# First feed-forward layers with the activations stationary: 60 of 88 pairs on one core

## The chip, the core and the metric

The kernel runs on one NeuronCore of a Trainium2 chip. The metric is device time in microseconds (us) from one launch, shorter is better. The kernel before takes 2496.74 us (median of three runs, 2496.37 to 2496.89). The engines named below are PE (TensorE, the matrix products; its weight loads have a row of their own, PEld), DVE (VectorE), ACT (ScalarE), POOL (GpSimd) and SP (SyncE, which issues most transfers).

## What is computed

One block of a model with 256 tokens and 2048 features: a feed-forward layer, a mixer (attention beside a gated delta rule), and a second feed-forward layer, each with an adaptive shift and scale before it and a gated residual and layer norm behind it. The change is in the feed-forward layers:

```
def swiglu_ffn(h, w_in, w_out):              # h [256, 2048], w_in [2048, 2 * 5632], w_out [5632, 2048]
    g, u = jnp.split(h @ w_in, 2, axis=-1)
    return (jax.nn.silu(g) * u) @ w_out
...
y = swiglu_ffn(x * (1.0 + scale[:, 0]) + shift[:, 0], w_ffn_in[l, 0], w_ffn_out[l, 0])
x = layer_norm(DEEPNORM_ALPHA * x + 0.5 * gate[:, 0] * y, ln_g[l, 0], ln_b[l, 0])
```

## The kernel before

**Numbers in two parts.** Every large product is made of three: an operand is split into a rounded part `hi` and a rest `lo`, and `mm3` (L145) issues hi·hi, hi·lo and lo·hi, one after the other, into one accumulator in PSUM; they stand in the profile as L147, L148 and L149. Weights come from HBM in chunks of 512 KB, `raw` [128, 1024]. ACT rounds a chunk to `hi` and DVE (in some stages POOL) subtracts to get `lo` (`_split`, L177). There are five `raw` buffers and three pairs of `hi` and `lo` (WB = 3), so the split of a chunk can start only when PE is through with the chunk three before it.

**Two forms of product.** `_wstat` (L274) keeps weights stationary: 128x128 weights are loaded into PE and 256 columns, all tokens of h^T, stream past them. A chunk is 24 such products, each with its own weight load. The result has features on the partitions. In the profile these are `mm<-h_hi,hi` and the like: out <- streaming operand, stationary operand. `_xstat` (L287) keeps activations stationary, 128 features by 128 tokens, and 512 weight columns stream. A chunk is 12 products, and the result has tokens on the partitions; two accumulators of [128, 512], one for each half of the tokens, fill side by side. In the profile these are `mx<-hi,hid`: the streaming weights first, then the stationary activations.

**Stages.** The hidden 5632 features of a feed-forward layer are 44 pairs of a gate block and an up block of 128 features. A layer runs in two halves (SIZES, L31: 28 and 16 pairs in layer 0, 22 and 22 in layer 2). A half first makes its pairs, then multiplies all of them with the second weights in `_y_blocks` (L702), in four blocks of 512 columns by `_xstat` with `hid` stationary. The first 28 pairs of layer 0 are made in a special way, by feature tiles as h becomes known (`start`, tiles `mms`), and do not change. The other 60 pairs are made by `_wstat`, four chunks a pair, tiles `mm`; two pairs of layer 2 (tiles `pre`) are made while the layer norm before it still produces h (`_Next.rest`, L569).

**Behind a pair.** `_ffn_hid_run` (L737) reads the pair's bank: ACT takes silu of the gate half (`sg`), DVE multiplies with the up half (`hidf`), ACT rounds to `hid` hi and DVE subtracts to `hid` lo. Features are on the partitions already, which is what `_y_blocks` wants of its stationary operand.

**Order.** It is set at build time: one main stream of products, and threads (`_Thread`, `spawn`) that put their instructions between them when a rough clock says that they are due. Each engine then runs its own list strictly in the order in which it was written. `weights` (L219) has the splits of the next two chunks written ahead of the products of a chunk. Four banks (`psm`) serve the main stream, and four (`pss`, tiles named `sm` in the code) serve threads. `_Ada` (L357) computes vectors for later parts between the products, on DVE, from 512 KB transfers of its own (`ar`): in layer 0 mostly reductions of 128x1024 against `crow`, in layer 2 sums into `acc` for one gate.

**Placement.** In both kernels the built program puts h (hi and lo) at byte 18016 and byte 34400 of each partition, behind the 4-byte tile `eps`; both are 32 past a multiple of 64. `hid`, `mgh`, `mgl`, `hi` and `lo` all start at multiples of 64.

Of the kernel before, what the change touches and what calls it, by code (L numbers as in the profile page):

```python
# [8 lines left out]
F32 = mybir.dt.float32  # L9
# [9 lines left out]
S = 256  # L19
# [11 lines left out]
SIZES = {0: (28, 16), 2: (22, 22)}  # L31
# [43 lines left out]
class _Engine:  # L75
    """An engine, with a rough clock of when it is through with what it was given."""
# [15 lines left out]
class _Kernel:  # L92
# [35 lines left out]
    def bank(self, shape, name):  # L128
        """A bank for a job of the main stream, when the thread that reads it last is through."""
        if len(self.users) == 4:  # L130
            th = self.users.pop(0)
            if th is not None:
                self.wait(lambda: th.done)
        self.users.append(None)
        return self.psm.tile(shape, F32, tag="mm", name=f"{name}{self.uid()}")

    def read(self, gen, back=1):
        """A thread that reads the newest bank (or the one back)."""
        th = self.spawn(gen)
        self.users[-back] = th  # L140
        return th

    # products
# [56 lines left out]
    def ahead(self, upto):  # L200
        """Emit loads and splits so that chunks up to upto are under way."""
# [9 lines left out]
    def hold(self, first, n):  # L211
        """The parts of n chunks go where h was."""
# [6 lines left out]
    def weights(self, held=0):  # L219
        """Parts of the next chunk; held: chunks before it whose products come later."""  # L220
# [27 lines left out]
def _rsqrt(k, pool, y, x, tag):  # L248
    """y = x ** -0.5 for small tiles: a guess from the exponent, then Newton's steps."""
# [9 lines left out]
def _products(k, ps, w, kt0, nkt, acts, first, last):  # L259
    """ps[:, b, :] += W[:, b]^T act, weights stationary, for nkt feature tiles."""  # L260
# [13 lines left out]
def _wstat(k, n, acts):  # L274
    """Two output blocks [128, 256] side by side in one bank, from n chunks."""
# [10 lines left out]

def _xstat(k, n, act, done, tail=0):  # L287
    """Natural [2][128 tok, 512]: activations stationary, weights moving; done: what reads it.

    tail: the last chunks go token tile by token tile and half by half (a bank for each), and are  # L290
    read at once."""
# [8 lines left out]
    def part(c, w, j, t, i):  # L300
        kt = 2 * c + j
        act.need(k, kt)
        lo, hi = halves[i]
        sl = slice(j * 512 + lo, j * 512 + hi)
        tk = slice(t * 128, (t + 1) * 128)
        k.mm3(pss[t][i][:, lo:hi], (_tile(act[0], kt)[:, tk], _tile(act[1], kt)[:, tk]), (w[0][:, sl], w[1][:, sl]),
              start=(kt == 0), stop=(kt == 2 * n - 1))
        k.pump()
# [25 lines left out]

def _ada_row(k, pool):
    """silu(c) along the columns of all partitions (in PSUM), from features on partitions."""
# [5 lines left out]
def _ada_keep(k):  # L342
    """The same in SBUF, for what comes later."""
# [6 lines left out]
def _ada_dot(k, raw, half, sub, kind, f, tmp, d):  # L350
    """One half of the sums for 128 features of a shift or a scale; features on partitions."""
# [83 lines left out]
class _More:  # L435
    """Shifts and scales whose weights are part of the weight stream."""
# [13 lines left out]
def _affine(k, sub, ln, shT, scT):  # L450
    """A = g (1 + scale), B = b (1 + scale) + shift, features on partitions."""
# [41 lines left out]
def _h_tile(k, pool, h, f, src, A, B):  # L493
    """h^T tile f = src * A + B, split in two parts."""
# [14 lines left out]

class _Ln:  # L510
    """Layer norm of x by rows: the statistics, and what comes of them."""
# [8 lines left out]
    def table(self):  # L520
        """Has the table of the square root there in time."""
# [7 lines left out]
    def factors(self, t):  # L529
        """1 / std, - mean / std and - mean."""  # L530
# [14 lines left out]
class _Next:  # L545
    """The layer norm, with x of it to DRAM and h of the next part, and that part's first products."""

    def __init__(self, k, idx, prep):
        self.k, self.idx, self.prep = k, idx, prep
# [19 lines left out]
    def rest(self, ln):  # L569
# [39 lines left out]
        th.step()  # L609
        acts = [h, h]  # L610
# [8 lines left out]
class _Last:  # L619
    """The layer norm of the result."""  # L620
# [4 lines left out]
    def load(self):  # L625
        """Thread: its vectors, for all tokens."""
# [36 lines left out]
def _load_x(k, a, pool, rows, tags, idx, delay, pace):  # L663
    """Thread: the residual from DRAM, with the affine part of the layer norm before it."""
# [22 lines left out]
def _residual(k, n, t, ps, lo, hi, gate, first, st):  # L687
    """x = (first: alpha) x + 0.5 gate y for columns lo..hi of 512; statistics if st."""
# [13 lines left out]
def _y_blocks(k, nchunk, act, ada, sub, first, ln, finish, tail):  # L702
    """y = act W2 by blocks of 512 columns, into x; with ln, also the layer norm after it."""
# [55 lines left out]

def _ffn(k, a, h, sub, items, interval, start, pre, finish, tail):  # L760
# [941 lines left out]
```

## Time and profile before

| | us |
|---|---|
| median of three runs | 2496.74 (2496.37 to 2496.89) |
| span of the profiled execution | 2501.1 |
| PE busy (products) | 2356.6, 94% |
| PEld busy (weight loads, beside PE) | 2230.8, 89% |
| DVE busy | 1747.1, 70% |
| ACT busy | 1037.8, 41% |
| POOL busy | 582.9, 23% |

The profile is of one execution of the program; its times are from the span's start. A product shows as busy from its first column to the modelled end of its last, so neighbours overlap: the pace of a stage is the distance from one start to the next, not the duration. The changed stages are from 565.81 to 750.13 us (16 pairs of layer 0), from 1723.99 to 1991.14 us (22 pairs of layer 2, the first two of them beside the layer norm) and from 2110.84 to 2364.29 us (the other 22).

### The profile page before, as it was taken

The numbers are of one execution on the slowest core, as the hardware profiler recorded it, in microseconds if no ns is written. First come the engines' busy times: TensorE is split into PE (matmuls) and PEld (weight loads), VectorE is DVE, ScalarE is ACT, GpSimd is POOL, SyncE is SP. The second block draws the span as 40 slices with busy tenths as digits, with TensorE's granted clock in tenths as the row PEclk, the third lists the DMA queues.
The fourth block names the chain that finished last, engine by engine and source line by source line (L and its number), as shares of the span: only waits on it lengthen the run. The fifth ranks groups of instructions, "written<-read, shape, count | busy, mean of one in ns | idle before, by whom it ended". The sixth has DMA issues, their size and how long they took to land. (4 is left out here: it accounts for less than half of the span.)

```text
span 2501.1 us, 42377 instructions
## 1 busy us (share of the span) xinstructions
PE 2356.6 (94%) x16989; PEld 2230.8 (89%) x16989; DVE 1747.1 (70%) x2436; ACT 1037.8 (41%) x1420; POOL 582.9 (23%) x320
## 2 busy tenths in 40 slices
PE   7999889789999889998988999998999999999997
PEld 7999887679998878898888999988999988999987
DVE  5767998577776567878686798786687555444456
ACT  4434334234443443444434434434444433444433
POOL 5885761000000443423334040004030000000001
PEclk8999999899999999999999999999999999999999
DMA  9998657788886555544445988885888665555553
GB/s 360 331 335 292 234 193 252 210 318 306 299 303 210 177 180 166 176 162 140 144 156 163 321 285 307 281 290 195 279 297 303 205 195 191 184 185 180 184 193 127
DMA packets 166245, 582.05 MB, mean 233 GB/s; under 512 B 19692, under 2 KB 22676, under 8 KB 165280
## 3 DMA queue, kind: packets, MB, share of 16 engines
q1 hardware_dynamic: 166048, 579.34, 68.3%
q8 instruction: 133, 2.18, 0.4%
q14 instruction: 64, 0.52, 0.1%
HBM read 571.41 MB, written 7.86 MB: 232 GB/s over the span
## 5 line engine op out<-in xcount | busy, mean ns | idle before, releaser
L88 ACT ACTIVATE hi<-raw 128x1024 fp32r<-128x1024 f32 x768 | 810.9, 1058 | 1019.1 <-PE mm L148 406.6
L88 DVE TENSOR_TENSOR lo<-raw,hi 128x1024 fp32r<-128x1024 f32 x587 | 735.7, 1257 | 507.7 <-ACT hi L88 504.3
L149 PE MATMUL mm<-h_hi,lo 128*128 128x256 f32 x3072 | 869.7, 283 | 19.1 <-DVE lo L88 19.0
L147 PE MATMUL mm<-h_hi,hi 128*128 128x256 f32 x3072 | 879.8, 286 | 0.0
L148 PE MATMUL mm<-h_lo,hi 128*128 128x256 f32 x3072 | 870.4, 283 | 0.0
L88 POOL TENSOR_TENSOR lo<-raw,hi 128x1024 fp32r<-128x1024 f32 x181 | 448.1, 2486 | 1030.3 <-ACT hi L88 1009.9
L149 PEld LDWEIGHTS mm<-h_hi,lo 128*128 128x128 f32 x3072 | 584.8, 190 | 21.1 <-DVE lo L88 20.7
L147 PEld LDWEIGHTS mm<-h_hi,hi 128*128 128x128 f32 x3072 | 582.3, 190 | 2.9 <-issue 2.5
L148 PEld LDWEIGHTS mm<-h_lo,hi 128*128 128x128 f32 x3072 | 582.6, 190 | 0.9 <-issue 0.6
L148 PE MATMUL mx<-lo,hid 128*128 128x512 f32 (+1 forms) x764 | 285.0, 373 | 25.3 <-DVE lo L88 23.5
L149 PE MATMUL mx<-hi,hid 128*128 128x512 f32 (+1 forms) x764 | 284.4, 372 | 0.0
L147 PE MATMUL mx<-hi,hid 128*128 128x512 f32 (+1 forms) x764 | 284.2, 372 | 0.1
L149 PE MATMUL mms<-h_hi,lo 128*128 128x256 f32 x896 | 258.9, 289 | 14.0 <-POOL lo L88 14.0
L147 PE MATMUL mms<-h_hi,hi 128*128 128x256 f32 x896 | 258.5, 288 | 9.6 <-ACT hi L88 6.5
L148 PE MATMUL mms<-h_lo,hi 128*128 128x256 f32 x896 | 256.7, 287 | 2.2 <-POOL h_lo L88 2.2
L148 PEld LDWEIGHTS mx<-lo,hid 128*128 128x128 f32 x764 | 144.8, 190 | 51.3 <-DVE lo L88 24.2
L88 DVE SCALAR_TENSOR_TENSOR acc<-ar,cs,acc 128x512 f32<-128x512 f32 x180 | 186.1, 1034 | 5.7 <-DMA ar<-in_w_gate_dram 2.0
L149 PEld LDWEIGHTS mms<-h_hi,lo 128*128 128x128 f32 x896 | 173.0, 193 | 15.7 <-POOL lo L88 15.7
L147 PEld LDWEIGHTS mms<-h_hi,hi 128*128 128x128 f32 x896 | 173.9, 194 | 10.7 <-ACT hi L88 7.5
L148 PEld LDWEIGHTS mms<-h_lo,hi 128*128 128x128 f32 x896 | 175.0, 195 | 2.7 <-POOL h_lo L88 2.5
L147 PEld LDWEIGHTS mx<-hi,hid 128*128 128x128 f32 x764 | 144.9, 190 | 26.0 <-issue 0.6
L149 PEld LDWEIGHTS mx<-hi,hid 128*128 128x128 f32 x764 | 144.9, 190 | 24.7
(295 smaller groups left out, 2578.0 us busy)
## 6 DMA issues: line engine op xcount, KB each, us to landing
raw<-in_w_ffn_in_dram SPq DMA_DIRECT2D x240, 512.0 KB, 4.2
raw<-in_w_ffn_out_dram SPq DMA_DIRECT2D x176, 512.0 KB, 4.3
raw<-in_w_first_dram SPq DMA_DIRECT2D x112, 512.0 KB, 4.5
ar<-in_w_gate_dram SPq DMA_DIRECT2D x96, 512.0 KB, 4.8
ar<-in_w_ada_dram SPq DMA_DIRECT2D x96, 512.0 KB, 5.1
sar<-in_w_ada_dram SPq DMA_DIRECT2D x64, 512.0 KB, 6.8
raw<-in_w_gab_dram SPq DMA_DIRECT2D x64, 512.0 KB, 4.8
raw<-in_w_kq_dram SPq DMA_DIRECT2D x32, 512.0 KB, 4.1
```

What stands on the lines that cost most here:

```text
L88: return f(*args, **kw)
L147: mm(ps, lhsT=lhs[0], rhs=rhs[0], start=start, stop=False, skip_group_check=True)
L148: mm(ps, lhsT=lhs[0], rhs=rhs[1], start=False, stop=False, skip_group_check=True)
L149: mm(ps, lhsT=lhs[1], rhs=rhs[0], start=False, stop=stop, skip_group_check=True)
```

## The change

60 pairs go from `_wstat` to `_xstat`. Four pairs make a block: 512 gate columns in eight chunks, then 512 up columns in eight chunks, with h stationary. The number of chunks (16 for four pairs) and of bytes stays. ACT takes silu of the two gate accumulators (`sg`, [128 tokens, 512] each), DVE multiplies `sg` in place with the up accumulators, and since tokens are now on the partitions, PE turns the product: eight transposes of 128x128 a block, in two groups of four into one bank each (`hT`). ACT rounds and DVE subtracts from there. The sizes of layer 2's halves go from 22 and 22 to 24 and 20, to be multiples of four. The host lays the weights out for the new form.

```
-SIZES = {0: (28, 16), 2: (22, 22)}
+SIZES = {0: (28, 16), 2: (24, 20)}
...
+def _ffn_block(k, h, hid, b, before, pre):
+    sg = {}
+    def gate(t, ps, lo, hi):
+        yield 0.2
+        while not all(th.done for th in before):
+            yield 0.3
+        sg[t] = k.hp.tile([128, 512], F32, tag=f"sg{t}", name=f"sg{k.uid()}")
+        k.A.activation(sg[t], ps, AF.Silu)
+    def up(t, ps, lo, hi):
+        yield 0.2
+        k.V.tensor_tensor(sg[t], sg[t], ps, ALU.mult)
+    def turn(ups):
+        while not all(th.done for th in ups):
+            yield 0.3
+        yield
+        for g in range(2):
+            ps = k.pss.tile([128, 2, S], F32, tag="sm", name=f"hT{k.uid()}")
+            for q in range(2):
+                for t in range(2):
+                    f = 2 * g + q
+                    k.tr(ps[:, q, t * 128:(t + 1) * 128], sg[t][:, f * 128:(f + 1) * 128])
+            yield
+            js = [4 * b + 2 * g + q for q in range(2)]
+            for q, j in enumerate(js):
+                both = k.hp.tile([128, 2, S], F32R, tag=f"hid{j}", name=f"hid{k.uid()}")
+                hid[0][j], hid[1][j] = both[:, 0, :], both[:, 1, :]
+                k.A.activation(hid[0][j], ps[:, q, :], AF.Copy)
+            yield
+            for q, j in enumerate(js):
+                k.V.tensor_tensor(hid[1][j], ps[:, q, :], hid[0][j].bitcast(F32), ALU.subtract)
+    if pre is None:
+        _xstat(k, KT // 2, h, gate)
+    else:
+        for t in range(2):
+            k.read(gate(t, pre[t], 0, 512), 2 - t)
+    _xstat(k, KT // 2, h, up)
+    th = k.spawn(turn(list(k.users[-2:])))
+    for i in range(4):
+        hid.job(4 * b + i, th)
+    return th
...
-            for j in range(j0, size):
-                ps = _wstat(k, 4, acts)
-                _ffn_hid(k, ps, hid, j)
+            turned = []
+            for b in range(b0, size // 4):
+                turned = [_ffn_block(k, h, hid, b, turned, None if b or half else pre)]
...
+        if self.wide:
+            pre = [k.bank([128, 512], "pre") for _ in range(2)]
+            for c in range(8):
+                w = k.weights()
+                for j in range(2):
+                    for t in range(2):
+                        _xprod(k, pre[t], w, h, 2 * c + j, j, t, 0, 512, KT - 1)
```

`_xprod` is the body of `_xstat`'s products under a name of its own: one `mm3` of 512 columns, then `pump`. The last part is in `_Next.rest`: the products beside the layer norm of layer 2 are now the first block's gate half.

**PE, the second half of layer 2.** Before, one pair ends and the next begins; nothing stands between them (`mm_22473` and `mm_22601` are two pairs' banks):

```order
L147 MATMUL mm_22473<-h_hi_18097,hi_22508 128x256
L148 MATMUL mm_22473<-h_lo_18098,hi_22508 128x256
L149 MATMUL mm_22473<-h_hi_18097,lo_22509 128x256
L147 MATMUL mm_22601<-h_hi_18097,hi_22541 128x256
L148 MATMUL mm_22601<-h_lo_18098,hi_22541 128x256
L149 MATMUL mm_22601<-h_hi_18097,lo_22542 128x256
```

Now, at the end of the third block of that half (`mx_21291` is its second up accumulator, `mx_21440` and `mx_21441` the next block's gate accumulators, or the first accumulators of `_y_blocks` behind a last block):

```order
L149 MATMUL mx_21291<-hi_21386,h_lo_17330 128x512
L147 MATMUL mx_21440<-hi_21404,h_hi_17329 128x512
L148 MATMUL mx_21440<-lo_21405,h_hi_17329 128x512
L149 MATMUL mx_21440<-hi_21404,h_lo_17330 128x512
L147 MATMUL mx_21441<-hi_21404,h_hi_17329 128x512
L148 MATMUL mx_21441<-lo_21405,h_hi_17329 128x512
L149 MATMUL mx_21441<-hi_21404,h_lo_17330 128x512
L147 MATMUL mx_21440<-hi_21404,h_hi_17329 128x512
L148 MATMUL mx_21440<-lo_21405,h_hi_17329 128x512
L149 MATMUL mx_21440<-hi_21404,h_lo_17330 128x512
L158 MATMUL hT_21459<-ident,sg_21304 128x128
L158 MATMUL hT_21459<-ident,sg_21306 128x128
```

Nine products of the next block stand between the block's last product and the first transpose; all products behind the transposes stand behind them on PE. The second group of transposes stands nine products later. It is so at all 15 blocks.

**DVE, the same place.** Before, around a pair's end (the multiplication writes `hidf`, and PE waits for nothing here):

```order
L88 TENSOR_TENSOR lo_22603<-raw_22447,hi_22602 128x1024
L88 TENSOR_TENSOR hidf_22625<-sg_22614,mm_22473 128x256
L88 TENSOR_TENSOR lo_22637<-raw_22478,hi_22636 128x1024
L88 TENSOR_TENSOR hid_22645<-hidf_22625,hid_22645 128x256
L88 TENSOR_TENSOR lo_22670<-raw_22512,hi_22669 128x1024
```

Now, at the end of the third block:

```order
L88 TENSOR_TENSOR lo_21387<-raw_21296,hi_21386 128x1024
L88 TENSOR_TENSOR lo_21405<-raw_21318,hi_21404 128x1024
L88 TENSOR_TENSOR lo_21423<-raw_21336,hi_21422 128x1024
L88 TENSOR_TENSOR lo_21443<-raw_21354,hi_21442 128x1024
L88 TENSOR_TENSOR sg_21304<-sg_21304,mx_21290 128x512
L88 TENSOR_TENSOR sg_21306<-sg_21306,mx_21291 128x512
L88 TENSOR_TENSOR lo_21472<-raw_21372,hi_21471 128x1024
L88 TENSOR_TENSOR hid_21467<-hT_21459,hid_21467 128x256
L88 TENSOR_TENSOR hid_21469<-hT_21459,hid_21469 128x256
```

`lo_21387` belongs to the up half's last chunk; the three behind it belong to the next three chunks. The two multiplications that the transposes read stand behind the split of the third next chunk, at all 15 blocks.

**DVE, layer 0.** At the third of layer 0's four blocks a reduction of `_Ada` also stands between that split and the multiplications (ISA is the reduction, and the read of its sum):

```order
L88 TENSOR_TENSOR lo_6651<-raw_6553,hi_6650 128x1024
L88 TENSOR_TENSOR lo_6671<-raw_6571,hi_6670 128x1024
L88 ISA ar_6608,ada_2780<-ar_6608,crow,tmp_6643 128x1024
L88 ISA ada_2780 128x1
L88 TENSOR_TENSOR sg_6514<-sg_6514,mx_6500 128x512
L88 TENSOR_TENSOR sg_6516<-sg_6516,mx_6501 128x512
```

At the other 14 blocks the split stands directly before the multiplications.

## Rows read from the trace of the kernel before

**Rows 1.** Page, part 1: busy us (share), instructions of each engine

```profile
PE 2356.6 (94%) x16989; PEld 2230.8 (89%) x16989; DVE 1747.1 (70%) x2436; ACT 1037.8 (41%) x1420; POOL 582.9 (23%) x320
```

**Rows 2.** Stages: window, length, PE PEld DVE ACT POOL, PEclk, DMA, GB/s

```profile
566.00:750.00 184.00, 184.00 (x1535) 184.00 (x1534) 141.11 (x182) 78.26 (x95) 0.00 (x0) 1.00 0.88 301
894.00:962.00 68.00, 58.15 (x266) 45.76 (x264) 54.27 (x97) 26.08 (x46) 29.80 (x28) 0.92 0.54 175
...
2111.00:2364.00 253.00, 253.00 (x2111) 253.00 (x2110) 124.35 (x134) 105.43 (x130) 0.00 (x0) 1.00 0.56 184
```

**Rows 3.** Timeline (start, us, engine, line): weights stationary, first product, first behind

```profile
2110.84 0.28 PE L147 MATMUL mm<-h_hi,hi 128*128 128x256 f32 x1
...
2364.29 0.39 PE L147 MATMUL mx<-hi,hid 128*128 128x512 f32 x1
```

**Rows 4.** Timeline: hid stationary, first and last product before rows 3

```profile
1991.14 0.39 PE L147 MATMUL mx<-hi,hid 128*128 128x512 f32 x1
...
2110.62 0.39 PE L149 MATMUL mx<-hi,hid 128*128 128x512 f32 x1
```

**Rows 5.** Timeline: h stationary in the mixer, an undisturbed stretch's first and last

```profile
920.99 0.39 PE L147 MATMUL mx<-hi,h_hi 128*128 128x512 f32 x1
...
927.31 0.39 PE L147 MATMUL mx<-hi,h_hi 128*128 128x512 f32 x1
```

**Rows 6.** Timeline: end of a 512-column block with hid stationary, in brackets waits

```profile
2050.78 0.39 PE L149 MATMUL mx<-hi,hid 128*128 128x512 f32 x1
...
2051.20 1.06 ACT L88 ACTIVATE hi<-raw 128x1024 fp32r<-128x1024 f32 x1 [1.66 <-PE mx L149]
...
2052.30 1.23 DVE L88 TENSOR_TENSOR lo<-raw,hi 128x1024 fp32r<-128x1024 f32 x1 [1.50 <-ACT hi L88]
...
2053.44 0.68 DVE L88 SCALAR_TENSOR_TENSOR res<-mx,gate 128x512 f32<-128x512 f32 x1
...
2054.23 0.69 DVE L88 SCALAR_TENSOR_TENSOR x<-x,res 128x512 f32<-128x512 f32 x1
...
2054.84 0.68 DVE L88 SCALAR_TENSOR_TENSOR res<-mx,gate 128x512 f32<-128x512 f32 x1
```

**Rows 7.** Timeline, mixer: transposes between 512-column products, eight unwaited, four after a wait

```profile
919.19 0.39 PE L149 MATMUL mx<-hi,h_lo 128*128 128x512 f32 x1
919.42 0.60 PE L158 MATMUL k<-ident,kq 128*128 128x128 f32 x4
919.86 0.60 PE L158 MATMUL q<-ident,kq 128*128 128x128 f32 x4
...
920.53 0.39 PE L148 MATMUL mx<-lo,h_hi 128*128 128x512 f32 x1
...
928.70 0.63 PE L158 MATMUL knT<-ident,kn 128*128 128x128 f32 x4 [0.31 <-DVE kn L88]
929.08 0.48 PE L147 MATMUL mx<-hi,h_hi 128*128 128x512 f32 x1
...
929.40 0.40 PE L148 MATMUL mx<-lo,h_hi 128*128 128x512 f32 x1
```

**Rows 8.** Instructions on tile ar: duration ns min/median/max, first and last start

```profile
L88 DVE CUSTOM_DVE_ANT_0 ar<-ar,crow,tmp x48: 1275/1278/2704, 464.5 to 1701.4; 128x1024 f32<-128x1024 f32 x48
```

**Rows 9.** Timeline, PE: products beside layer 2's layer norm, undisturbed from here, and end

```profile
1734.46 0.36 PE L147 MATMUL pre<-h_hi,hi 128*128 128x256 f32 x1
...
1755.06 0.28 PE L147 MATMUL mm<-h_hi,hi 128*128 128x256 f32 x1
```

**Rows 10.** Timeline, PE, mixer: products after waits of two lengths

```profile
1064.63 0.58 PE L149 MATMUL mm<-h_hi,lo 128*128 128x256 f32 x1 [3.71 <-DVE lo L88]
...
1067.69 0.28 PE L148 MATMUL mm<-h_lo,hi 128*128 128x256 f32 x1
...
1137.74 0.39 PE L149 MATMUL mm<-h_hi,lo 128*128 128x256 f32 x1 [1.47 <-DVE lo L88]
1137.96 0.28 PE L147 MATMUL mm<-h_hi,hi 128*128 128x256 f32 x1
```

More of the change, by code (lines that the diff above doesn't have):

```diff
@@ L284, in _tile, with _xprod @@
     return part[kt] if isinstance(part, dict) else part[:, kt, :]
+def _xprod(k, ps, w, act, kt, j, t, lo, hi, last):
+    act.need(k, kt)
+    sl = slice(j * 512 + lo, j * 512 + hi)
+    tk = slice(t * 128, (t + 1) * 128)
+    k.mm3(ps[:, lo:hi], (_tile(act[0], kt)[:, tk], _tile(act[1], kt)[:, tk]), (w[0][:, sl], w[1][:, sl]),
+          start=(kt == 0), stop=(kt == last))
+    k.pump()
 def _xstat(k, n, act, done, tail=0):
@@ L300, in part @@
     def part(c, w, j, t, i):
-        kt = 2 * c + j
-        act.need(k, kt)
         lo, hi = halves[i]
[L304 to L308, printed above, removed]
+        _xprod(k, pss[t][i], w, act, 2 * c + j, j, t, lo, hi, 2 * n - 1)
     more = max(0, tail - WB)
@@ L545, with __init__ @@
 class _Next:
-    def __init__(self, k, idx, prep):
-        self.k, self.idx, self.prep = k, idx, prep
+    def __init__(self, k, idx, prep, wide):
+        self.k, self.idx, self.prep, self.wide = k, idx, prep, wide
     def step(self, stage, ada, ln):
@@ L609, in rest @@
         th.step()
+        if self.wide:
[5 more added lines that the diff above has]
+                        _xprod(k, pre[t], w, h, 2 * c + j, j, t, 0, 512, KT - 1)
+            k.wait(lambda: th.done)
+            return h, pre
         acts = [h, h]
@@ L769, in _ffn @@
             hid.ready = size
-            j0 = 0
+            b0 = 0
             if half == 0:
@@ L780, in _ffn @@
                 if start is not None:
-                    j0 = size
+                    b0 = size // 4
                     ada = start(h, hid, side)
@@ L786, in _ffn @@
                 else:
-                    j0 = len(pre)
-                    for j in range(j0):
-                        _ffn_hid(k, pre[j], hid, j, back=j0 - j)
                     ada = side()
-            for j in range(j0, size):
-                ps = _wstat(k, 4, acts)
-                _ffn_hid(k, ps, hid, j)
+            turned = []
+            for b in range(b0, size // 4):
+                turned = [_ffn_block(k, h, hid, b, turned, None if b or half else pre)]
             res = _y_blocks(k, size // 2, hid, ada, sub, half == 0, ln if half else None, finish, tail)
@@ L1464, in tile_hybrid_block @@
         j0 = 0
-        if sub == 1:
-            plan += [a["w_ffn_in"][sub, j, c] for c in range(4) for j in range(2)]
-            j0 = 2
         for half, size in enumerate(SIZES[2 * sub]):
             if sub or half:
-                plan += [a["w_ffn_in"][sub, j, c] for j in range(j0, NPAIR if half else size) for c in range(4)]
-            j0 = SIZES[2 * sub][0]
+                plan += [a[f"w_ffn_in{sub}"][i, b, c] for b in range(j0, j0 + size // 4) for i in range(2)
+                         for c in range(KT // 2)]
+                j0 += size // 4
             plan += [a[f"w_ffn_out{sub}{half}"][n, c] for n in range(4) for c in range(size // 2)]
@@ L1568, in prep1 @@
         return _affine(k, 2, 1, d[(2, 0)], d[(2, 1)])
-    h, pre = _ffn(k, a, h, 0, FFN_ADA, FFN_PACE, start, None, _Next(k, 0, prep0), TAIL)
-    h, pre = _mixer(k, a, h, pre, lambda pool: _Ada(k, a, pool, TAIL_ADA, TAIL_PACE), _Next(k, 1, prep1))
+    h, pre = _ffn(k, a, h, 0, FFN_ADA, FFN_PACE, start, None, _Next(k, 0, prep0, False), TAIL)
+    h, pre = _mixer(k, a, h, pre, lambda pool: _Ada(k, a, pool, TAIL_ADA, TAIL_PACE), _Next(k, 1, prep1, True))
     last = _Last(k, a, out)
@@ L1647, in _layout @@
     wi = g["w_ffn_in"].reshape(2, D, 2 * DFF)
+    for sub in range(2):
+        j0 = (NPAIR if sub else SIZES[0][1]) * 128
+        r[f"w_ffn_in{sub}"] = np.stack([chunks_x(wi[sub][:, DFF * i - j0:DFF * i]) for i in (1, 2)])
     wi = [pair(w[:, :DFF], w[:, DFF:]) for w in wi]
-    r["w_ffn_in"] = np.stack([chunks_w(w, 2) for w in wi])
     first = []
```

1 line of the change is left out of this document (removed).

## The prediction

> **What bounds the kernel now.** I read the busy shares first, then the stages, then single products. PE is busy 94% of the span, DVE 70%, ACT 41% [rows 1]. The stages say more: from 566 to 750 us and from 2111 to 2364 us, two of the stretches that change, PE is busy all the time at full granted clock, while DVE has 141.11 of 184 us and 124.35 of 253 us, and transfers run at 0.88 and 0.56 [rows 2]. So PE sets the time there: what PE saves is saved, and what PE newly waits for is lost, unless another engine was late anyway.
>
> The duration of a product says nothing of its pace; the distance between starts does. With weights stationary, 2112 products of 256 columns take 2364.29 - 2110.84 = 253.45 us, 0.1200 us each, 0.2400 us for 512 columns [rows 3]. For 512 columns with activations stationary the trace has two paces, and they differ. With `hid` stationary, 527 steps take 2110.62 - 1991.14 = 119.48 us, 0.2267 us each [rows 4]. With h stationary, in the mixer, 27 steps take 927.31 - 920.99 = 6.32 us, 0.2341 us each, at the full clock too [rows 5]. The changed products are the second sort: same function, same h, same shapes.
>
> **The change, part by part.**
>
> *Products.* 60 pairs are 240 chunks: 240 x 24 = 5760 products of 256 columns become 2880 of 512. At the pace of h, each pair of old products saves 0.2400 - 0.2341 = 0.0059 us; in all 2880 x 0.0059 = **17.0 us saved**. At the pace of `hid` it would be 2880 x 0.0133 = 38.3 us. I take 17.0, because rows 5 are the same instruction with the same operand. Their stage differs (POOL is busy there [rows 2]), and that is why I keep 38.3 as the other end.
>
> [...]
>
> *The wait for the multiplications* is the large term. Call the start of a block's last product 0. Rows 6 show such an end: 2050.78 is product 264 from 1991.14, the last of a block. ACT can round the third next chunk only once that product has freed its buffers, and starts 0.42 us after it; DVE's split starts at 1.52, and the next DVE operation at 2.66, reading the finished accumulator. In the changed kernel two multiplications of 512 columns stand there. One takes 0.68 us (`res`, also 512 columns out of PSUM), and an independent second one starts 0.61 us behind the first (2054.23 to 2054.84 [rows 6]). So the second ends at 2.66 + 0.61 + 0.68 = 3.95. PE meets the transposes after nine products, at 10 x 0.234 = 2.34, and the second transpose needs that second multiplication. Nothing else can run meanwhile: all later products stand behind.
>
> A group of four transposes behind a wait has its next product 0.38 us after its start and the one after that 0.32 us later (928.70 to 929.40) [rows 7]. The first transpose is through earlier, so three are left, 0.27 instead of 0.38 (0.11 for one: four take 919.42 to 919.86). The second product behind them starts at 3.95 + 0.05 + 0.27 + 0.32 = 4.59, 0.05 being an estimate for the hand-over, instead of 11 x 0.2341 = 2.58: 2.01 us late. The second group waits for nothing. Eight unwaited transposes put the second product behind them at 920.53 instead of 919.19 + 0.47: 0.87 us, so 0.44 for four. That makes 2.01 + 0.44 = 2.45 us a block, x 15 = **36.8 us lost**. Bounds: were the multiplications early, only 0.87 x 15 = 13 us would remain; an error of 0.4 us in the wait is 6 us.
>
> *Layer 0's third block.* A reduction of 1.28 us and the read of its sum (together 1.4) stand ahead of the multiplications [rows 8]: **1.4 us lost**; the other blocks' reductions have DVE's gap ahead of the split (1.50 us [rows 6]). If they come late, each costs as much; I allow 3.
>
> *Beside the layer norm.* From 1734.46 to 1755.06 us 57 of the 64 groups of three run undisturbed [rows 9]; seven ran between waits for h. Now there are 32 groups, twice as long. If seven are again done between the waits, 25 x 3 x 0.2341 = 17.6 us remain, starting up to 7 x 0.34 = 2.4 us later. The stage then ends 3.0 to 0.6 us sooner, of which 0.5 is counted above. I take **0.9 us saved**, with bounds of -2.5 and 0.
>
> *Behind a block.* ACT and DVE do less per four pairs: two operations of 512 and four of 256 columns each, instead of eight of 256. Those that turn `hT` into `hid` hide under DVE's idle quarter and half [rows 2]; their reader comes at least one block later, or, for a last block, at the end of a column block. After the wait the split is not late: the next chunk's buffers are free three products behind the transposes, and two chunks are ready. At zero, then; without that cover it would be a wait of about 1 us a block. Bytes and queues are as before. The new sizes of layer 2 move one boundary by two pairs; nothing waits at it. Zero.
>
> Sum: -17.0 + 36.8 + 1.4 - 0.9 = **+20.3 us**. The profiled execution has a span of 2501.1 us, 4.4 over the median; I add the sum to the median: 2496.7 + 20.3 = **2517 us**, and would expect some 2521 as a span.
>
> **The rivals.**
>
> *The pace of hid, no change.* If the mixer, and not h, makes rows 5 slow, the saving is 38.3. The wait grows by the 0.08 us that PE is there sooner: 2.53 x 15 = 38.0. Sum +0.2 with the small terms: 2497 us. [...] Against it: the pace holds through the whole stretch, while POOL is busy only part of the time [rows 2]. 14%.
>
> *No wait, faster.* If the multiplications end before 2.34 us, only the transposes remain: -17.0 + 13.1 - 0.9 = -4.8, 2492 us, and with the pace of `hid` 2471 us. It decides at the third next split: that split would have to be over at about 1 us, and it starts at 1.52 [rows 6]. The order has it ahead of the multiplications at all 15 blocks. 6%.
>
> *The clock falls, slower still.* [...] 6%.
>
> **How the numbers follow.** The forecast as summed has 74%, 2508 to 2526 by its own bounds (0.4 us a block, 3 us for late reductions, the layer norm). The range reaches down to the case of no change and up over late reductions at several blocks: 2497 to 2532, which leaves out the faster case, most of the clock's, and the edge of the others. A measurement of this kernel can tell about 0.2%, 5 us. Faster by more than that: 7%. Within: 13%. Slower: 80%.
>
> **What would show it.** In the changed profile: products `mx<-hi,h_hi` 0.234 apart in the FFN stages (0.227 would be the first rival); 15 waits of `hT` for a DVE `sg`, about 1.2 us of idle PE each; the multiplication starting about 2.7 us after the block's last product; the granted clock at 1.00 in these stages. A stage of layer 0 of 4 x (192 x 0.2341 + 2.45) = 190 us instead of 184 shows the sum at once. I am wrong if those waits are short, or if the pace is that of `hid`.

## The result, and the profile after

The changed kernel takes 2526.91 us (median of four runs, 2524.41 to 2528.56), beside 2496.55 us for the kernel before (four runs, 2494.27 to 2496.89): a ratio of 1.0113, 95% interval 1.0101 to 1.0125, or 30.4 us more at the medians. The profiled execution has a span of 2526.8 us, 25.7 more than that of before. The forecast was 2517 us, slower.

First the page's part 1, answering to [rows 1] (busy us, share and number of instructions of each engine):

```profile
PE 2357.3 (93%) x14217; PEld 2087.3 (83%) x14217; DVE 1741.7 (69%) x2406; ACT 1034.5 (41%) x1390; POOL 581.4 (23%) x320
```

PE is as busy as before, with a sixth fewer instructions. So nearly all that was added is time in which PE stands still. The stages by windows (length, then busy time of PE, PEld, DVE, ACT, POOL, then granted clock, DMA share and GB/s), answering to [rows 2]:

```profile
566.73:755.26 188.53, 183.79 (x794) 146.84 (x792) 138.80 (x171) 76.70 (x85) 0.00 (x0) 1.00 0.87 297
1740.50:2030.60 290.10, 278.15 (x1181) 221.22 (x1180) 190.74 (x199) 119.67 (x141) 32.48 (x23) 0.98 0.77 257
...
2163.80:2398.60 234.80, 230.01 (x994) 183.75 (x993) 110.65 (x108) 94.55 (x106) 0.00 (x0) 1.00 0.58 180
```

They are layer 0's 16 pairs, layer 2's first 24 and its last 20. In the first and the last the clock stays at 1.00 and PE idles nearly 5 us, where before it had no gap at all; in the middle one it idles 12 us, and the clock is not always up. (Layer 0's stage is 188.53 us and not 190: the wait and the transposes of its last block fall behind its end.)

The pace: the timeline's rows of PE for the second product behind a block's transposes and for the last product of the next block, 172 steps later:

```profile
2358.03 0.40 PE L148 MATMUL mx<-lo,h_hi 128*128 128x512 f32 x1
...
2398.32 0.39 PE L149 MATMUL mx<-hi,h_lo 128*128 128x512 f32 x1
```

(2398.32 - 2358.03) / 172 = 0.2342 us a product, as in [rows 5], not the 0.2267 of [rows 4]. And a block's end, the one before (start, duration, engine, line, operation; in brackets what it idled for and on whom):

```profile
2350.87 0.40 PE L149 MATMUL mx<-hi,h_lo 128*128 128x512 f32 x1
...
2351.31 1.06 ACT L88 ACTIVATE hi<-raw 128x1024 fp32r<-128x1024 f32 x1 [1.75 <-PE mx L149]
...
2352.40 1.23 DVE L88 TENSOR_TENSOR lo<-raw,hi 128x1024 fp32r<-128x1024 f32 x1 [1.59 <-ACT hi L88]
...
2352.99 0.39 PE L149 MATMUL mx<-hi,h_lo 128*128 128x512 f32 x1
2353.54 1.28 DVE L88 TENSOR_TENSOR sg<-sg,mx 128x512 f32<-128x512 f32 x2
2354.37 0.30 PE L158 MATMUL hT<-ident,sg 128*128 128x128 f32 x1 [0.99 <-DVE sg L88]
2354.87 0.55 PE L158 MATMUL hT<-ident,sg 128*128 128x128 f32 x3 [0.21 <-DVE sg L88]
...
2355.49 0.40 PE L148 MATMUL mx<-lo,h_hi 128*128 128x512 f32 x1
```

Read from the block's last product, 2350.87: ACT's rounding at +0.44, DVE's split at +1.53, the multiplications from +2.67 to +3.95, PE's ninth product at +2.12, and the second product behind the transposes at +4.62, where the working gave 4.59. PE idles 0.99 + 0.21 us for `sg`. Twelve of the other blocks read the same within 0.1 us. From one block's end to the next the last stage takes 2398.32 - 2350.87 = 47.45 us; four pairs took 384 x 0.1200 = 46.08 before [rows 3].

The two blocks that differ are layer 0's third, where the reduction stands ahead of the multiplications as forecast:

```profile
706.37 0.40 PE L149 MATMUL mx<-hi,h_lo 128*128 128x512 f32 x1
...
709.05 1.28 DVE L88 CUSTOM_DVE_ANT_0 ar<-ar,crow,tmp 128x1024 f32<-128x1024 f32 x1
...
710.25 1.28 DVE L88 TENSOR_TENSOR sg<-sg,mx 128x512 f32<-128x512 f32 x2
711.08 0.30 PE L158 MATMUL hT<-ident,sg 128*128 128x128 f32 x1 [2.20 <-DVE sg L88]
```

(the multiplications start at +3.88 instead of +2.67, 1.21 us later), and layer 2's third, which the forecast did not have:

```profile
1876.65 2.56 DVE L88 SCALAR_TENSOR_TENSOR acc<-ar,cs,acc 128x512 f32<-128x512 f32 x2
1879.13 3.48 DVE L88 TENSOR_TENSOR lo<-raw,hi 128x1024 fp32r<-128x1024 f32 x2
...
1881.68 0.39 PE L149 MATMUL mx<-hi,h_lo 128*128 128x512 f32 x1
...
1882.53 2.43 DVE L88 SCALAR_TENSOR_TENSOR acc<-ar,cs,acc 128x512 f32<-128x512 f32 x2
...
1884.37 1.71 POOL L88 TENSOR_TENSOR x<-x,rowg 128x512 f32<-128x512 f32 x1
1884.88 2.28 DVE L88 TENSOR_TENSOR lo<-raw,hi 128x1024 fp32r<-128x1024 f32 x1
1886.16 2.13 POOL L88 TENSOR_TENSOR x<-x,rowb 128x512 f32<-128x512 f32 x1
1887.08 1.27 DVE L88 TENSOR_TENSOR sg<-sg,mx 128x512 f32<-128x512 f32 x2
1887.81 1.50 PE L158 MATMUL hT<-ident,sg 128*128 128x128 f32 x4 [3.64 <-DVE sg L88]
...
1889.54 0.63 PE L148 MATMUL mx<-lo,h_hi 128*128 128x512 f32 x1
...
1894.48 0.39 PE L149 MATMUL mx<-hi,h_lo 128*128 128x512 f32 x1
```

There DVE's split starts at +3.20 instead of +1.53, behind two sums that take 2.43 us together, and lasts 2.28 us instead of 1.23, while POOL works on x. The multiplications start at +5.40 instead of +2.67. PE waits 3.64 us for `sg` and runs on at the lower level of its clock (granted 0.52 on average from 1887.81 to 1894.48; a product takes 0.63 us and the next starts 0.43 later) until the upper one (granted 1.00, a product 0.39) is back at 1894.48. What that costs shows in the distance between block ends:

```profile
1781.31 0.40 PE L149 MATMUL mx<-hi,h_lo 128*128 128x512 f32 x1
...
1829.25 0.39 PE L149 MATMUL mx<-hi,h_lo 128*128 128x512 f32 x1
...
1935.00 0.40 PE L149 MATMUL mx<-hi,h_lo 128*128 128x512 f32 x1
```

From the first to the second of these it is 47.94 us; from 1881.68 to 1935.00 it is 53.32, 5.4 us more.

### The profile page after: what moved, and what is told of

Its sections match the earlier page's. It is cut to its first block, busy times and chain, and to the rows that moved or that the text cites. A ratio compares the mean times of both kernels' runs of the same rounds, so it can differ in the third digit from the quotient of the medians.

```text
span 2526.8 us, 36799 instructions
## 1 busy us (share of the span) xinstructions
PE 2357.3 (93%) x14217; PEld 2087.3 (83%) x14217; DVE 1741.7 (69%) x2406; ACT 1034.5 (41%) x1390; POOL 581.4 (23%) x320
## 5 line engine op out<-in xcount | busy, mean ns | idle before, releaser
L147 PE MATMUL mx<-hi,h_hi 128*128 128x512 f32 x992 | 399.1, 402 | 0.0
L148 PE MATMUL mx<-lo,h_hi 128*128 128x512 f32 x992 | 395.4, 399 | 0.0
L149 PE MATMUL mx<-hi,h_lo 128*128 128x512 f32 x992 | 395.2, 398 | 0.0
L149 PE MATMUL mm<-h_hi,lo 128*128 128x256 f32 x1216 | 347.5, 286 | 21.3 <-DVE lo L88 21.2
L147 PE MATMUL mm<-h_hi,hi 128*128 128x256 f32 x1216 | 353.6, 291 | 0.0
L148 PE MATMUL mm<-h_lo,hi 128*128 128x256 f32 x1216 | 345.3, 284 | 0.0
L148 PE MATMUL mx<-lo,hid 128*128 128x512 f32 (+1 forms) x760 | 284.2, 374 | 25.7 <-DVE lo L88 23.9
L149 PEld LDWEIGHTS mm<-h_hi,lo 128*128 128x128 f32 x1216 | 231.4, 190 | 24.1 <-DVE lo L88 23.5
L147 PEld LDWEIGHTS mm<-h_hi,hi 128*128 128x128 f32 x1216 | 232.9, 192 | 2.7 <-issue 2.6
L148 PEld LDWEIGHTS mm<-h_lo,hi 128*128 128x128 f32 x1216 | 232.2, 191 | 0.6 <-issue 0.6
L148 PEld LDWEIGHTS mx<-lo,h_hi 128*128 128x128 f32 x992 | 188.7, 190 | 44.9 <-POOL lo L88 0.4
```

Of the source, the lines that this page charges most:

```text
L147: mm(ps, lhsT=lhs[0], rhs=rhs[0], start=start, stop=False, skip_group_check=True)
L148: mm(ps, lhsT=lhs[0], rhs=rhs[1], start=False, stop=False, skip_group_check=True)
L149: mm(ps, lhsT=lhs[1], rhs=rhs[0], start=False, stop=stop, skip_group_check=True)
```

## The experiments

My theory of the +25.7 us: 17 us saved on products, 37 lost in waiting for the multiplications and in the transposes, and some 5 lost once where DVE is slow. Rivals: that the pace of 0.234 is an accident of where h lies, and that PE's lost time is set by something else and would come back as another wait. Where a run moves h, its start is that of the built program. The three runs that put h at a multiple of 64 also move what lies further on by 64 bytes: hi, lo and raw then start 64 past a multiple of 512 instead of at one, hid 320 past one instead of 256. In all other runs these keep their offsets within 512 bytes, but for two that move hi and lo by 256 and say so.

**The wait: transposes later.**

```
         while not all(th.done for th in ups):
             yield 0.3
         yield
+        yield 2.2
         for g in range(2):
```

> The changed kernel with the transposes of each block 12 products later (21 instead of 9 products behind the block's last one); the second group stays nine products behind the first. Theory wait (of the 2.04 us a block by which the product behind the first transposes is late, 1.60 is waiting for DVE's two multiplications and 0.44 the transposes): the multiplications end 3.95 us behind the block's last product, the transposes now stand at 22 x 0.2343 = 5.15, so no wait is left and 15 x 1.60 = 24 us are saved; the long wait at layer 2's third block, behind which the granted clock fell, becomes short too, worth some 5 us more: 2527 - 24 to 29 = 2498 to 2503 us. Rival given back (the time that PE gains is lost at once at the next split or at a bank, since DVE and ACT are through with the block later): less than 10 us are saved, 2517 us or more, and a new wait of 1 us or more stands behind each block.

Measured: 2497.54 us (ten runs, 2492.23 to 2500.55), beside 2499.05 for the kernel before on the same chip: a ratio of 0.999 (0.998 to 1.000), half a microsecond under the range of the theory. The span is 2494.7 us, 32.1 under that of the changed kernel. The same block end in the timeline:

```profile
2322.01 0.40 PE L149 MATMUL mx<-hi,h_lo 128*128 128x512 f32 x1
...
2323.54 1.22 DVE L88 TENSOR_TENSOR lo<-raw,hi 128x1024 fp32r<-128x1024 f32 x1 [1.59 <-ACT hi L88]
...
2324.68 1.28 DVE L88 TENSOR_TENSOR sg<-sg,mx 128x512 f32<-128x512 f32 x2
...
2326.93 0.40 PE L149 MATMUL mx<-hi,h_lo 128*128 128x512 f32 x1
2327.16 0.60 PE L158 MATMUL hT<-ident,sg 128*128 128x128 f32 x4
...
2327.83 0.40 PE L148 MATMUL mx<-lo,h_hi 128*128 128x512 f32 x1
```

DVE does the same at the same distances (+1.53, +2.67), and the transposes at +5.15 have no bracket: nothing waits. Block ends lie 45.86 us apart instead of 47.45, so 1.59 us a block is the wait, 23.9 in all, and 45.86 - 192 x 0.2343 = 0.87 the transposes alone, both as worked out. No new wait stands behind the block, and none of the time was given back. At layer 2's third block PE does not wait either, and the clock stays up there (products of 0.39 and 0.40 us from 1869.42 to the transposes at 1874.58).

**The slow block: POOL's work earlier.** `_load_x` of layer 2 starts 12 us earlier, in the changed kernel:

```
-                    k.spawn(_load_x(k, a, k.lnp, k.lnp, ("x0", "x1"), *((1, 40.0, X_PACE) if sub else (None, 0.0, 3.0))))
+                    k.spawn(_load_x(k, a, k.lnp, k.lnp, ("x0", "x1"), *((1, 28.0, X_PACE) if sub else (None, 0.0, 3.0))))
```

> The changed kernel with the loading of x in layer 2 (POOL's affine work on it) started 12 us earlier. At the end of layer 2's third block PE waits 3.64 us for the multiplications instead of 1.1 to 1.3, and runs on at the lower clock. Theory POOL (DVE's operations take up to twice as long while POOL works on x: a split 2.28 us instead of 1.23 there; POOL's work, now ending at about 1888 us, would be over before 1877): the wait at that block becomes one of 1.1 to 1.3 us, the clock stays at its upper level there, and 4 to 8 us are saved: 2519 to 2523 us. Rival transfer (DVE is late because the sums for the gate wait for their 512 KB transfers, whatever POOL does): the long wait stays at that block, 2527 us within 3.

Measured: 2521.32 us (2518.42 to 2522.33; ratio 1.0096, 1.0079 to 1.0113), 5.6 less than the changed kernel; the span is 10.2 less, 5.4 of it between this block's end and the next (47.91 us instead of 53.32). POOL's last operation now ends at 1870.2 us, and the third block's end reads:

```profile
1876.97 0.40 PE L149 MATMUL mx<-hi,h_lo 128*128 128x512 f32 x1
...
1878.50 1.23 DVE L88 TENSOR_TENSOR lo<-raw,hi 128x1024 fp32r<-128x1024 f32 x1
...
1879.64 1.28 DVE L88 TENSOR_TENSOR sg<-sg,mx 128x512 f32<-128x512 f32 x2
1880.38 0.33 PE L158 MATMUL hT<-ident,sg 128*128 128x128 f32 x1 [0.91 <-DVE sg L88]
1880.97 0.55 PE L158 MATMUL hT<-ident,sg 128*128 128x128 f32 x3 [0.27 <-DVE sg L88]
```

The split is back at +1.53 and 1.23 us, the wait at 1.18 (0.91 + 0.27), and the clock stays up (from the second product behind it on 0.39 and 0.40 us each): the rival that the long wait would stay falls. x's own transfers moved with POOL's work, so this run alone does not tell the two apart; the rows of the changed kernel do. From 1876.65 us to the multiplications DVE is never idle there, so neither pair of sums waited for its transfer. Its two pairs of sums and three splits take 10.75 us in all; at the 1.53 and 1.23 us that a pair and a split take in the run with POOL's work earlier it would be 6.75, and these 4.0 us are more than the 2.73 by which the multiplications were late. The two intervals of the ratio overlap (1.0101 to 1.0125 for the changed kernel); it is the rows that decide.

**The pace: h at a multiple of 64.** `eps` is widened to 64 bytes, and `lam` behind h to 64 as well; h moves by 32 bytes and all that lies behind `lam` by 64:

```
-    k.eps = pp.tile([128, 1], F32, tag="eps", name="eps")
+    k.eps = pp.tile([128, 16], F32, tag="eps", name="eps")[:, 0:1]
...
-    k.lam = k.pp.tile([128, 1], F32, tag="lam", name="lam")
+    k.lam = k.pp.tile([128, 16], F32, tag="lam", name="lam")[:, 0:1]
```

> The changed kernel with h put 32 bytes later in each partition, so that it starts at a multiple of 64 as hid does; order and instructions stay. Theory address (the products with h stationary are slow because h starts 32 past a multiple of 64): their pace falls from 0.2343 to that of hid, 0.2267. There are 2880 of them, so 2880 x 0.0076 = 22 us are saved; the ten products in front of each of the 15 waits only make the wait longer, 15 x 10 x 0.0076 = 1 us is lost again: 2527 - 21 = 2506 us. Rival operand (it is not the address but something else about h, such as its two parts lying 16 KB apart where those of hid lie 1 KB apart, or the stage): the pace stays at 0.2343 and the time at 2527 us within 4.

Measured: 2512.71 us (2507.06 to 2514.26; ratio 1.0050, 1.0033 to 1.0067). Some 14 us are saved, but not where the theory put them. With h stationary, 27 steps:

```profile
2300.08 0.40 PE L147 MATMUL mx<-hi,h_hi 128*128 128x512 f32 x1
...
2306.38 0.39 PE L147 MATMUL mx<-hi,h_hi 128*128 128x512 f32 x1
```

6.30 / 27 = 0.2333, an eighth of the way to 0.2267. With hid stationary, now 320 past a multiple of 512, the pace stays at 0.2267. The gain is where h streams: the start of layer 0 is 10 us shorter and the mixer 6. 51 steps of that start:

```profile
100.16 0.28 PE L147 MATMUL mms<-h_hi,hi 128*128 128x256 f32 x1
...
105.94 0.28 PE L147 MATMUL mms<-h_hi,hi 128*128 128x256 f32 x1
```

5.78 / 51 = 0.1133 instead of 0.1200. The kernel before, with the same edit, shows the gain alone:

> The kernel before with h at a multiple of 64: there h streams past stationary weights in nearly all products, and is stationary only in 96 x 3 products of the mixer's dv. Theory address, for stationary tiles alone: 288 x 0.0076 = 2 us or less, so the same within the measurement, 2495 to 2497 us, and the pace of 256 columns stays at 0.1200. Rival every read (the address slows a streaming operand as much as a stationary one): the 256-column pace falls by about 0.007 too, and with some 10,000 such products the time falls by some 50 us or more.

Measured: 2477.47 us (2476.41 to 2479.85; ratio 0.9908, 0.9893 to 0.9923). The first product of the last 22 pairs, and the first one behind them, answering to [rows 3]:

```profile
2089.07 0.28 PE L147 MATMUL mm<-h_hi,hi 128*128 128x256 f32 x1
...
2337.82 0.40 PE L147 MATMUL mx<-hi,hid 128*128 128x512 f32 x1
```

248.75 / 2112 = 0.1178 instead of 0.1200. Both theories put down beforehand miss: the place counts where h streams too, at a third of the size that the rival gave it. Since hi and lo move here as well, the run does not show whether h's own start does it.

Both edits together:

> Both edits in the changed kernel: h at a multiple of 64, and the transposes 12 products later. If both theories hold, the sums add up: 22 us for the pace (nothing of it goes into a wait now) and 24 to 29 us for the wait, 2527 - 46 to 51 = 2476 to 2481 us, some 17 us under the kernel before. If address falls and wait holds: 2498 to 2503 us. If wait falls and address holds: 2506 us.

Measured: 2481.00 us (2476.07 to 2485.39; ratio 0.9921, 0.9902 to 0.9939). The time is the one expected, but partly for the wrong reason: 16.5 us for the placement against the run with late transposes alone, and of 12.8 us between the two spans 8.3 lie in the start and the mixer, where h streams. From 25 to 200 us, where h streams, the pace is 0.1178 here and 0.1133 in the run with the placement alone, though every tile lies at the same place in both.

**The pace: h at 256 past a multiple of 512.** h starts 96 past a multiple of 512 in both kernels and 128 past one in the runs above; hid and the mixer's `mgh` and `mgl`, whose pace is 0.2267, start 256 past one (320 in the three runs above). `eps` is widened to 192 bytes and `lam` to 384, so that what lies behind moves by a whole 512:

```
-    k.eps = pp.tile([128, 1], F32, tag="eps", name="eps")
+    k.eps = pp.tile([128, 48], F32, tag="eps", name="eps")[:, 0:1]
...
-    k.lam = k.pp.tile([128, 1], F32, tag="lam", name="lam")
+    k.lam = k.pp.tile([128, 96], F32, tag="lam", name="lam")[:, 0:1]
```

> The kernel with the late transposes, and h moved by 160 bytes, so that each of its 512-byte stationary tiles starts 256 past a multiple of 512, as those of hid and of mgh do, whose pace is 0.2267. (With h at a multiple of 64, at 128 past a multiple of 512, the pace with h stationary was 0.2333.) Theory offset (the offset within 512 decides, 64 was only too small a unit): the pace with h stationary falls to 0.2267, 2880 x 0.0076 = 22 us in the changed stages, and the stages with h streaming gain as well as they did at a multiple of 64: 2497 - 22 and less, 2460 to 2476 us. Rival not the offset: the pace with h stationary stays between 0.231 and 0.235, and the time is that of the run with both edits, 2476 to 2485 us, or more.

Measured: 2480.98 us (2477.51 to 2481.36; ratio 0.9930, 0.9916 to 0.9945). With h stationary, 27 steps:

```profile
2319.67 0.39 PE L147 MATMUL mx<-hi,h_hi 128*128 128x512 f32 x1
...
2325.79 0.39 PE L147 MATMUL mx<-hi,h_hi 128*128 128x512 f32 x1
```

6.12 / 27 = 0.2267: exactly the pace of hid. The five blocks of the last stage take 221.5 us instead of 228.4. Together the changed stages are 17.6 us shorter than in the profile with late transposes alone; the theory had 22. So the pace is the theory's, but the time is above its range and inside the rival's: the lower part of the range needed the gain where h streams, and there the pace is 0.1200 again. The kernel before in that place:

> The kernel before with h in the same place, 256 past a multiple of 512. At a multiple of 64 its pace with weights stationary went from 0.1200 to 0.1178 and the time to 2477.5 us. Theory offset: the same or better, 0.1133 to 0.1178 a product of 256 columns; at 0.1133 in the 4224 products of the two largest changed stages alone 19 us less, and 2440 to 2478 us in all. Rival (y streams from tiles at 256 past a multiple of 512, and its products are 0.1200 apart): the gain is lost again, 0.1200 and 2497 us.

Measured: 2498.93 us (2496.72 to 2504.09; ratio 1.0009, 1.0000 to 1.0018), 0.1200 a product: the rival holds.

The part of memory does not count (h at 96 past a multiple of 512, transposes late; two pads that keep the offsets are left out here):

```
-    k.pp = pp = ctx.enter_context(tc.tile_pool(name="pp", bufs=1))
...
     k.rawp = ctx.enter_context(tc.tile_pool(name="rawp", bufs=RAWB))
     k.wp = ctx.enter_context(tc.tile_pool(name="wp", bufs=WB))
...
+    k.pp = pp = ctx.enter_context(tc.tile_pool(name="pp", bufs=1))
```

> The kernel with the late transposes, with the raw, hi and lo buffers ahead of h in the partition (h then starts at byte 63584 instead of 18016, hi at 37376 instead of 80384), every tile at the same offset within 512 as before. Theory offset: the pace with h stationary stays at 0.2343 and the time at 2497 us within 5. Rival region (which part of the memory h lies in decides, against that which weights are written to and streamed from): the pace changes, by up to the 0.0076 to that of hid, 2475 us, or the other way.

Measured: 2497.49 us (2495.42 to 2501.30; ratio 0.9998, 0.9989 to 1.0008), against 2497.54 without that move, and the pace stays at 0.2344.

Nor does a move of the weights by 256 bytes count:

```
+    pad0 = ctx.enter_context(tc.tile_pool(name="pad0", bufs=1)).tile([128, 64], F32, tag="pad", name="pad0")
+    nc.vector.memset(pad0, 0.0)
     k.wp = ctx.enter_context(tc.tile_pool(name="wp", bufs=WB))
...
```

> The kernel before with its hi and lo buffers 256 bytes later, so that the stationary tiles of its weight-stationary products start 256 past a multiple of 512 instead of at one; h stays where it was, at 96 past one. Theory stationary offset (256 past a multiple of 512 is good for a stationary tile, whatever streams): the pace of 256 columns goes from 0.1200 to that of half a 512-column product of hid, 0.1133; over the 12,300 products with weights stationary that is up to 82 us, 2415 to 2440 us. The pace of 512 columns with hid stationary, whose streaming weights move by 256 too, stays at 0.2267. Rival difference (what counts is how the two tiles lie to each other: hid at 256 against weights at 0 is good): now hid and weights both lie at 256, and the pace with hid stationary rises from 0.2267 towards 0.234 (2280 products, 17 us); that of 256 columns changes little: 2497 to 2515 us.

Measured: 2498.97 us (2491.44 to 2500.99; ratio 0.9998, 0.9988 to 1.0008). Both theories miss: 256 columns stay at 0.1200, and 512 with hid stationary at 0.2267.

> The kernel with the late transposes and h at 256 past a multiple of 512 (2481 us), with hi and lo 256 bytes later too. Theory stationary offset: h stationary stays at 0.2267, and the weight-stationary products that are left (some 6,300 of h, and those of the mixer's output) go from 0.1200 to 0.1133, 42 us or more: 2430 to 2445 us. Rival difference: h and hid stationary rise from 0.2267 towards 0.234, (2880 + 2280) x 0.0076 = 39 us, 2481 to 2520 us.

Measured: 2477.00 us (2475.66 to 2481.91; ratio 0.9915, 0.9900 to 0.9930): h stationary 0.2267, h streaming 0.1200, as without the move of the weights. Both theories miss here too. What counts may still be how the two operands lie to each other: a move by 256 leaves their distance the same past a multiple of 256, and no run moves the weights alone by less.

**Towards a faster version.** h in two places, by tiles of 128 more elements and a view that starts 32 elements later in layer 2 (`eps` is of 64 bytes, `lam` of 512; hi, lo and hid keep their offsets):

```
-        h = _new_h(k)
+        h = _new_h(k, 32 if self.wide else 0)
...
```

> The kernel with the late transposes; h at 128 past a multiple of 512 where most of its products stream it (layer 0 and the mixer), and at 256 past one in layer 2, where it is only stationary. If the offset of h alone sets the pace, the times of the two runs that had one of these offsets throughout add up by stages: the start and the mixer as at 128 (256 columns 0.1178 apart), layer 2 as at 256 (512 columns 0.2267 apart instead of 0.231 to 0.233, 11 blocks x 192 products x 0.0045 to 0.0066 = 10 to 14 us under the 2481 us of the run at 128): 2467 to 2471 us, under both kernels and under the kernel before at 128 (2477.5). If the pace hangs on something that only went along with the offset, the time is 2477 to 2483 us.

Measured: 2475.43 us (2472.55 to 2476.20; ratio 0.9907, 0.9891 to 0.9924). Layer 2's two feed-forward stages are 10 us shorter than with h at 128, as expected; of that 5.6 us show at the median, since 256 columns are not 0.1178 apart in this run. 51 steps of the start:

```profile
100.06 0.28 PE L147 MATMUL mms<-h_hi,hi 128*128 128x256 f32 x1
...
106.11 0.28 PE L147 MATMUL mms<-h_hi,hi 128*128 128x256 f32 x1
```

6.05 / 51 = 0.1186, and it stays near that up to the end of the mixer. So h's start alone does not set the pace: it is 128 past a multiple of 512 here as in the three runs above. What differs is that hi and lo lie at a multiple of 512 here and 64 past one there, and that the two parts of h lie 512 bytes further apart; no run tells these two apart. Another offset, 192, with `eps` of 128 bytes and `lam` of 448, in a single run:

> The kernel with the late transposes and h at 192 past a multiple of 512, to see which other offsets are good. Known so far, 512 columns with h stationary: 0.2343 at 96, 0.2333 at 128, 0.2267 at 256; 256 columns with h streaming: 0.1200 at 96, 0.1178 at 128, 0.1200 at 256. If the stationary tile wants a multiple of 256, the first is 0.231 or more here; if the streaming tile only wants to be off a multiple of 256 by a multiple of 64, the second is 0.1178 or less and the time about that of the run at 128, 2481 us; if it wants 128 itself, 0.1200 and 2497 us.

Measured: 2461.21 us (one run; before 2496.13 to 2506.48 beside it), the fastest of all. 51 steps with h streaming at the start, and 27 with h stationary:

```profile
100.10 0.28 PE L147 MATMUL mms<-h_hi,hi 128*128 128x256 f32 x1
...
105.88 0.28 PE L147 MATMUL mms<-h_hi,hi 128*128 128x256 f32 x1
...
2299.65 0.39 PE L148 MATMUL mx<-lo,h_hi 128*128 128x512 f32 x1
...
2305.83 0.39 PE L148 MATMUL mx<-lo,h_hi 128*128 128x512 f32 x1
```

5.78 / 51 = 0.1133 and 6.18 / 27 = 0.2289. Neither stationary nor streaming h wants exactly what the runs before suggested. How much of this time is the offset is open: it is one run, and the start can run at 0.1133 or at 0.1178 with every tile at the same place, as the two runs of the changed kernel with h at a multiple of 64 show. What the runs show of the places, beside each other:

| h starts past a multiple of 512 by | hi and lo by | 512 columns, h stationary | 256 columns, h streaming | form of before, us | changed form, transposes late, us |
|---|---|---|---|---|---|
| 96 | 0 | 0.2343 | 0.1200 | 2499.05 | 2497.54 |
| 96 | 256 | 0.2341 (in the mixer) | 0.1200 | 2498.97 | not run |
| 128 | 64 | 0.2333 | 0.1133 to 0.1178 | 2477.47 | 2481.00 |
| 128 (in layer 2 256) | 0 | 0.2324 to 0.2333 (0.2267) | 0.1186 | not run | 2475.43 |
| 192 | 0 | 0.2289 | 0.1133 to 0.1178 | not run | 2461.21 (one run) |
| 256 | 0 | 0.2267 | 0.1200 | 2498.93 | 2480.98 |
| 256 | 256 | 0.2267 | 0.1200 | not run | 2477.00 |

So the changed form, its wait taken away, is level with the form of before at 96 and at 128 (hi and lo at 64), and 18 us faster at 256.

## Why the prediction was right, step by step

| term | forecast, us | measured in the profiled execution, us |
|---|---|---|
| products | -17.0 | 15 x (46.08 - 192 x 0.2342) = -16.7 |
| wait and transposes | +36.8 | 15 x (47.45 - 44.97) = +37.2 |
| layer 0's third block | +1.4 | +1.2 |
| beside the layer norm | -0.9 | -1.1 |
| behind a block, boundary of layer 2's halves | 0 | 0 |
| layer 2's third block | not in the sum | +5.4 |
| sum | +20.3 | +26.0, of 25.7 in the spans |

**Products.** The choice of 0.2341 over 0.2267 was right, and so was its ground, the same operand in [rows 5]. It is not the mixer but the placement: the run with h at 256 has the pace of `hid` in the same instructions, and its changed stages are 17.6 us shorter. So the rival "pace of hid" was false of this program and is true of another placement.

**The wait.** The reading of [rows 6] held to 0.03 us. The 0.05 us for the hand-over was the author's estimate; in the profile after, the second multiplication ends at 2354.82 and the transposes that need it start at 2354.87. And the run with late transposes shows its two parts apart, 1.59 and 0.87 us a block, where the working gave 1.6 and 0.87. That run is also the rival "no wait", which the order of instructions excluded here: it comes out at 2497.54, 1.5 us under the kernel before beside it, where the working gave 4.8.

**The mis-sized step** is "if they come late, each costs as much; I allow 3", together with the clock. I looked for late multiplications in layer 0, where the reductions are, and took DVE's slack in layer 2 from the last stage, where POOL is idle [rows 2]. In the first half of layer 2 POOL works on x for 38 us, DVE's operations take longer beside it (a split 2.28 us instead of 1.23), and one of the six block ends falls into that time. The rival "the clock falls" then came true at one block of 15, and at the other 14 not (from the second product behind the wait on 0.39 and 0.40 us each). I had waits of 1.47 and 3.71 us to go by [rows 10]; now a wait of 2.20 us is followed by products at the upper level (0.39 us, layer 0's third block) and one of 3.64 by products at the lower (0.63 us). The length of the wait alone does not tell, as the kernel before shows in its first half of layer 2:

```profile
1862.39 0.50 PE L153 MATMUL aps<-acclo,ones 128*128 128x512 f32 x1 [1.66 <-DVE acclo L88]
...
1863.24 0.41 PE L147 MATMUL mm<-h_hi,hi 128*128 128x256 f32 x1
```

There 0.41 instead of 0.28 us is the lower level (granted 0.50 from 1863.24 to 1866.22), behind a wait of 1.66 us. (The same product waits 2.73 us in the changed kernel, with the lower level behind it too, 0.63 us a product and granted 0.50 from 1867.09 to 1870.08.) Of the 5.4 us at layer 2's third block 2.7 are the transposes' later start (+6.13 us instead of +3.41), and the other 2.7 come behind it, where the clock is down (granted 0.52).

**Beside the layer norm.** From the last product of the mixer's last stage to the last of the first four pairs it is 59.11 us instead of 61.28. Of these 2.2 us, 1.1 are the products' own.

**What was left over.** At the medians the loss is 30.4 us, 4.7 more than between the two profiled executions, since that of before was a long one of its kernel (its mixer, which does not change, is 2.2 us longer than in the changed kernel's); the interval of the ratio, 25.2 to 31.2 us, holds both. That is why the time lies 10 us over the forecast, though the terms leave 5.4.

## What to carry to other kernels

Where a result must go back through PE, count what stands ahead of it on the engine that prepares it: here the split of the third next chunk, 1.23 us, and two multiplications cost 1.59 us a block, and one line that puts twelve more products ahead of the transposes took it all away. Look for other engines' work in each stage before taking a duration from a quieter one. And before two forms of a product are compared, compare them at several placements of the operand that they treat differently: with one and the same form, a move of h (in three runs by 32 bytes, with the weights by 64) changed the time of the whole kernel by 16 to 22 us, in a single run by 36.

## What the runs showed of the hardware

**The pace of a product changed with where its operands start.** With the products the same, 512 columns took 0.2343, 0.2333, 0.2289 or 0.2267 us with h stationary at 96, 128, 192 or 256 bytes past a multiple of 512, and 256 columns 0.1133 to 0.1200 with h streaming. Moving the weights by 256 (256 columns 0.1200 us, 2498.97 us in all), or h to another part of the memory at the same offset (512 columns 0.2344, 2497.49 us), changed nothing. It is not shown that the start of one operand alone decides. With h at 128, 256 columns took 0.1186 us with the weights at 0 and 0.1133 to 0.1178 with them at 64; and `hid` kept 0.2267 when it went from 256 to 320 together with the weights, from 0 to 64. The distance of the two operands past a multiple of 256 would fit all rows with 512 columns as well; no run tests it alone. With 512 columns the runs differ by up to 7.6 ns a product. Why some places are slow is open, and so is why with every tile at one place a stretch runs at 0.1133 and another at 0.1178: with h at 128 the products of the form of before ran at 0.1133 in most of the time from 1789 to 1863 us and at 0.1178 in nearly all of the rest.

**DVE's operations took longer beside POOL's.** A split of 1.23 us took 2.28 while POOL worked on x, and a pair of sums 2.43 instead of 1.53 (at the same place with POOL's work earlier). The split's extra 1.05 us is within the length of one POOL operation beside it (1.71 and 2.13 us); why it is longer is not shown.
